# A decoder layer's mixer: the recurrence's gates of three chunks moved together behind the third query product

## The chip, the cores and the metric

The kernel runs on one core of one Trainium2 chip. The metric is the device time of one execution in microseconds (us). Before the change the median of 3 runs is 843.24 us (842.97 to 843.72). One more execution was profiled; it took 842.55 us, and its profile spans 840.8 us. Times inside the profile are counted from the start of that span.

Engines are named as in the profile: PE (TensorE matmuls), PEld (TensorE weight loads), DVE (VectorE), ACT (ScalarE), POOL (GpSimd), SP (SyncE, which here only issues DMAs). L1456 is line 1456 of the kernel before.

## The reference, cut to what matters

One layer: a half-step gated FFN, a mixer and a second half-step gated FFN, each between two RMS norms and added to the residual. SEQ is 512, D_MODEL 1024, float32 throughout. The mixer projects its input with one matrix `w_in` into the recurrence's input, its gate, and queries, keys and values, and runs two things side by side:

```python
def rg_lru(x_in, conv_w, conv_b, w_rg, b_rg, w_ig, b_ig, lam):
    xc = causal_depthwise_conv(x_in, conv_w, conv_b)
    r = jax.nn.sigmoid(block_diag(xc, w_rg, b_rg).astype(jnp.float32))
    i = jax.nn.sigmoid(block_diag(xc, w_ig, b_ig).astype(jnp.float32))
    log_a = LRU_C * r * jax.nn.log_sigmoid(lam.astype(jnp.float32))
    a = jnp.exp(log_a)
    mult = jnp.sqrt(-jnp.expm1(2.0 * log_a))
    u = mult * (i * xc.astype(jnp.float32))
    ...
    _, h = lax.associative_scan(combine, (a, u), axis=1)
```

and a sliding-window attention of 8 heads with 2 key/value heads (window 128, blocks of 128 queries, a sink term in the softmax). Both results are normed, joined and multiplied by `w_o`. The recurrence has 512 channels, four chunks of 128; `w_rg` and `w_ig` are block diagonal with blocks of 64.

## The kernel before, in words

**Layout and products.** Activations stand with channels on the 128 partitions and the 512 tokens along the free axis, so one chunk of 128 channels is one tile of 128x512. A float32 product is made of three matmuls: each operand is split into a rounded high part (a cast on ACT) and a low part (a subtraction on DVE or POOL), and high*high, high*low and low*high are summed in PSUM (`mm3`, L503 to L508). A projection chunk is eight such triples (`product`, L510), 24 matmuls into one PSUM bank. Weights come in by DMA (L175, on SP), are cast on ACT (L210, `whi`) and subtracted on DVE or POOL (L215, `wlo`); `W.take` hands them out and issues casts and loads some units ahead.

**What sets the order.** The schedule is by hand: each engine executes its instructions in the order in which the code issues them, and semaphores make an instruction wait for its inputs and for its output buffer. An engine whose next instruction waits does nothing else in the meantime. Buffers come from pools that are handed round in turn: 8 PSUM banks (`bank`), 38 tiles of 2 KB per partition (`t2k`), and 8 working buffers (`wt`). A tile asked for from a pool waits for the last reader of the buffer that it gets.

**The stage of the change** lies between 370 and 416 us. In order of the code:

- `in_product("pk")` and `in_product("pv")`: the products for keys and values. `conv_in` and `conv` (L1433, L1439) make the convolved chunks `xc` of the recurrence, on ACT and DVE.
- A loop over j = 0 to 3 with one query product `pq` each (24 matmuls). In the loop before the change follow, in this order: `split_xc(j + 1)` (L1472: `xch`, a cast on ACT, and `xcl`, a subtraction on POOL), `lru_gates(j)`, and `in_parts` for the queries (L1485).
- `lru_gates(ci)` (L1450) runs six matmuls of 64 rows by 512 columns, in pairs that use two halves of the array at once, into the banks `rg` and `ig`. ACT applies the sigmoid to each bank (`r`, L1458, and `other`, L1460). The tile `r` holds on its upper partitions the half that belongs to the other gate, so SP copies two halves into the buffer `ig` by DMA (L1459, L1461), POOL multiplies `xc` by it in place (L1463, the group `xc<-ig,xc`), and a DMA from POOL's queue puts the other half of the decay gate into `r` (L1464). The tile `th` is only asked for here; the decay writes it later.
- `in_parts` for query j (L1485): DVE scales the bank (`qT`, L1428), copies its first 128 columns to `home` (L1488), ACT casts the high part (`qT0h`, ..., L1494; for j = 3 the tile is a quarter of `attn`), and DVE subtracts the low part (`qT0l`, ..., L1495). For j = 3 that subtraction is put off (`deferred`, L186).
- After j = 0, PE transposes the values (`vt`, L1514) and DVE copies them to `home` (L1516).

Then attention begins: `preload(AF.Exp)` loads another function table on ACT (L482), and `products(0)` (L1598) multiplies the first block's queries and keys, straight from `home`: four steps of two matmuls, step j on the columns that query j was copied to. DVE masks the scores and takes the maxima, ACT takes the exponentials, PE transposes them (`pt`, L1653) and multiplies them by the values (`po`, L1676). Between these, PE works off the 96 matmuls of the gate projection (`gt`, `pump`), and ACT and DVE the decay of the recurrence: `decay_a` (L1561) writes `th`, `r` and `m`, `decay_b` (L1568), `root`, `root_u` and `scan` follow.

The function table for the sigmoid is loaded in front of the first sigmoid in ACT's order (the row ACT_TABLE_LOAD at L1458). The queue of SP is in order, and so is POOL's; POOL issues its DMAs itself, between its computations.

Of the kernel before, what the change touches and what calls it, by code (L numbers as in the profile page):

```python
# [23 lines left out]
KC = C // P  # L24
# [98 lines left out]
def tile_layer(ctx: ExitStack, tc: tile.TileContext, out: bass.AP, **ins: bass.AP):  # L123
    nc = tc.nc
    pe, dve, act, pool, sync = nc.tensor, nc.vector, nc.scalar, nc.gpsimd, nc.sync
# [14 lines left out]
    SIDE = [slice(0, HD), slice(HD, P)]  # L140

    def bank(name):
        return psum.tile([P, T], F32, tag="bank", name=name)

    def t2k(name, dt=F32):
        return big.tile([P, T], dt, tag="t2k", name=name, bufs=NT2K)
# [16 lines left out]
    def wt(name, w=T, dt=F32):  # L163
        return tmp.tile([P, w], dt, tag="w", name=name, bufs=NW)
# [5 lines left out]
    def load_raw(srcs, nk, w, name):  # L170
        raw = wpool.tile([P, nk * w], F32, tag="raw", name=f"raw_{name}", bufs=NRAW).rearrange("p (k c) -> p k c", k=nk)
        o = 0
        for src in srcs:
            n = src.shape[1]
            sync.dma_start(raw[:, :, o:o + n], src.rearrange("(k p) c -> p k c", p=P))  # L175
            o += n
        return raw
# [215 lines left out]
    for g, (f0, f1) in enumerate(GROUPS2):  # L393
        if g == 0:
            for f in range(f0, f1, 2):
                add_gate_up(w2, f, "b")
            r = W.raw(lambda f=f0: load_raw([ins["ffn2_w_down"][0, f * P:(f + 2) * P, :]], 2, D, f"bd{f}"))
# [40 lines left out]
    for i in range(2):  # L438
        load_x(0, i)
        for o in (0, F):  # L440
            r = first_raw[o, i] = t2k(f"first{o}{i}").rearrange("p (k c) -> p k c", k=4)
# [9 lines left out]
    for name, n in ROWS:  # L451
        if name in ("b_rg", "b_ig"):

            j = name == "b_ig"
# [37 lines left out]
    def col(name, i):  # L492
        return colrange(name)[:, i:i + 1]
# [930 lines left out]
    def in_product(name, hooks=(), ahead=AHEAD):  # L1424
        return product(W.take(ahead), mx.xs, name=name, hooks=hooks)
# [2 lines left out]
        dve.tensor_mul(t, b, R)  # L1428
        return t

    xcs, th, rs_, us_ = [], [], [], []

    def conv_in(ci, b):  # L1433
        xp = wt(f"xp{ci}", T + 4)
# [15 lines left out]
    def lru_gates(ci):  # L1450

        banks = bank(f"rg{ci}"), bank(f"ig{ci}")
        (hi, lo), (xh, xl) = gw["both"], xc_parts[ci]
        for i, (w, x) in enumerate(((hi, xh), (hi, xl), (lo, xh))):
            for ps, half in zip(banks, SIDE):
                pe.matmul(ps, w[half, ci, :], x[half, :], start=i == 0, stop=i == 2)  # L1456
        r, other, ig = t2k(f"r{ci}"), wt(f"other{ci}"), wt(f"ig{ci}")
        act.activation(r, banks[0], AF.Sigmoid, bias=col("b_rg", ci))  # L1458
        sync.dma_start(ig[SIDE[0], :], r[SIDE[1], :])  # L1459
        act.activation(other, banks[1], AF.Sigmoid, bias=col("b_ig", ci))  # L1460
        sync.dma_start(ig[SIDE[1], :], other[SIDE[0], :])  # L1461
        u = xcs[ci]
        pool.tensor_mul(u, ig, u)  # L1463
        pool.dma_start(r[SIDE[1], :], other[SIDE[1], :])  # L1464
        t = t2k(f"th{ci}")
        rs_.append(r)
        us_.append(u)
        th.append(t)

    xc_parts = {}  # L1470

    def split_xc(ci):  # L1472
        xh, xl = wt(f"xch{ci}", T, F32R), wt(f"xcl{ci}", T, F32R)
        act.copy(xh, xcs[ci])
        pool.tensor_sub(xl, xcs[ci], xh.bitcast(F32))
        xc_parts[ci] = xh, xl
# [8 lines left out]
    def in_parts(b, first, name, low=dve):  # L1485

        x = scaled(wt(name), b)
        dve.tensor_copy(first, x[:, :P])  # L1488
        if name == "qT3":
            spare.extend(fours("attn", F32R))  # L1490
            xh, xl = spare.pop(), spare.pop()
        else:
            xh, xl = t2k(f"{name}h", F32R), t2k(f"{name}l", F32R)
        act.copy(xh, x)  # L1494
        low.tensor_sub(xl, x, xh.bitcast(F32))  # L1495
        return xh, xl
# [7 lines left out]
    qT = []  # L1504
    for j in range(4):
        b = in_product(f"pq{j}")
        if j < KC - 1:
            split_xc(j + 1)
        lru_gates(j)
        qT.append(in_parts(b, q0[:, j * P:(j + 1) * P], f"qT{j}", deferred if j == 3 else dve))  # L1510
        if j == 0:
            vt = bank("vt")
            for b in range(NB):
                pe.transpose(vt[:, b * P:(b + 1) * P], vT[:, b * P:(b + 1) * P], ident)  # L1514
            v = home[0][:, P + 2 * T:P + 2 * T + 8 * (HD + 1)]
            dve.tensor_copy(v.rearrange("p (h d) -> p h d", d=HD + 1)[:, :, :HD], vt.rearrange("p (h d) -> p h d", d=HD))  # L1516
# [528 lines left out]
```

## Time and profile before

| | |
|---|---|
| median of 3 runs | 843.24 us (842.97 to 843.72) |
| profiled execution, its own time | 842.55 us |
| its span in the profile | 840.8 us |
| PE busy | 832.2 us (99%) |
| DVE busy | 723.8 us (86%) |
| ACT busy | 520.9 us (62%) |
| POOL busy | 162.6 us (19%) |

Busy time of an engine is the union of its instructions. In the lists in order of time each row has the start in us, the length in us, the engine, the source line, the operation, what it writes and reads, its shape and a count where equal rows are merged; a bracket gives the idle time of the engine just before and what ended it. Buffer numbers are left out of the names: `qT` stands for four tiles, one after the other. On ACT and DVE the start of an instruction can lie about 0.1 us before the end of the one ahead, since two overlap a little.

### The profile page before, as it was taken

Reading aid. Unit: us, or ns where it says so; the run is one execution under the profiler, and the core shown is the slowest. Engines: PE = TensorE matmul, PEld = TensorE weight load, DVE = VectorE, ACT = ScalarE, POOL = GpSimd, SP = SyncE. Lnnn points to the kernel's source line nnn. Section 1 sums busy time; section 2 is a strip of 40 time slices with the busy share of each in tenths; the row PEclk is TensorE's granted clock in tenths of the full one; section 3 lists DMA queues with packets and bytes.
Section 4 is the critical chain, followed back from the end, with each engine's and each line's share of the span. In section 5 each row is a group of like instructions: output and inputs, shape, how many; then the busy total and the mean of one; then the engine's idle time right before and its main releaser. Section 6 shows DMA issues by size and latency. Waiting matters only on the chain.

```text
span 840.8 us, 12378 instructions
## 1 busy us (share of the span) xinstructions
PE 832.2 (99%) x4504; PEld 718.9 (85%) x4504; DVE 723.8 (86%) x1026; ACT 520.9 (62%) x821; POOL 162.6 (19%) x178
## 2 busy tenths in 40 slices
PE   9999999999999999999999999999999999999996
PEld 8988888988988998987788899888888888888885
DVE  4978999998989965879889589799999899898996
ACT  6646756666666655556797456536758667666562
POOL 2023000140320333304531052002004114032001
PEclk9999999999999999999999999999999999999999
DMA  7249429398595799323511131169439939769842
GB/s 252 77 128 347 135 79 318 80 251 267 123 255 186 167 261 331 93 62 108 157 51 51 51 105 47 50 129 290 179 106 232 317 92 257 253 149 258 305 140 101
DMA packets 123614, 143.73 MB, mean 171 GB/s; under 512 B 23897, under 2 KB 81569, under 8 KB 123041
## 3 DMA queue, kind: packets, MB, share of 16 engines
q1 hardware_dynamic: 109232, 111.86, 42.0%
q0 software_dynamic: 14176, 30.94, 17.0%
q8 instruction: 35, 0.57, 0.3%
q14 instruction: 27, 0.21, 0.1%
q10 hardware_dynamic: 144, 0.13, 0.0%
HBM read 100.45 MB, written 40.89 MB: 168 GB/s over the span
## 4 chain that ended last, share of the span: by engine, by line
PE 96%; DVE 2%; DMA 1%; SPq 0%; issue 0%; ACT 0%; DVEq 0%; ACTq 0%
PE aa L951 10%; PE ab L951 10%; PE db L951 5%; PE da L951 5%; PE yaa L1347 3%; PE bb L951 3%; PE ba L951 3%; PE yda L1347 2%; PE ya L506 2%; PE ya L507 2%; PE ya L508 2%; PE aa L881 1%; PE a_first L1206 1%; PE yab L1884 1%; PE yab L1885 1%; PE yab L1886 1%
## 5 line engine op out<-in xcount | busy, mean ns | idle before, releaser
L1116 POOL DMA_DIRECT2D yp_a<-stage x42 | 36.8, 1064 | 182.6 <-ACT stage L1113 158.8
L1116 POOL DMA_DIRECT2D yp_b<-stage x42 | 36.4, 1084 | 144.3 <-ACT stage L1113 117.8
L506 PE MATMUL ya<-hha,whi_ad 128*128 128x512 f32 x62 | 24.1, 389 | 0.0
L507 PE MATMUL ya<-hla,whi_ad 128*128 128x512 f32 x62 | 24.1, 389 | 0.0
L508 PE MATMUL ya<-hha,wlo_ad 128*128 128x512 f32 x62 | 24.1, 389 | 0.0
L686 POOL TENSOR_TENSOR acca_r<-acca_r,sq_r 128x512 f32<-128x512 f32 x6 | 8.1, 1357 | 61.7 <-ACT sq_r L536 61.7
L1900 POOL DMA_DIRECT2D yp_b<-stage x8 | 4.3, 548 | 67.1 <-ACT stage L1899 67.1
L524 PE MATMUL an<-xh_mx,whi_xl 128*128 128x256 f32 x64 | 15.9, 289 | 0.0
L525 PE MATMUL an<-xh_mx,wlo_xl 128*128 128x256 f32 x64 | 15.5, 283 | 0.0
L2003 POOL TENSOR_TENSOR last<-yp,grow 128x512 f32<-128x512 f32 x3 | 3.9, 1290 | 57.2 <-DVE yp L1993 57.2
L2000 ACT ACTIVATE ysq<-yp 128x512 f32<-128x512 f32 (+1 forms) x8 | 4.8, 606 | 16.2 <-DVE yp L1993 16.2
L506 PE MATMUL gt<-xh_mx,whi_gt 128*128 128x512 f32 x32 | 14.3, 445 | 0.0
L508 PEld LDWEIGHTS ya<-hha,wlo_ad 128*128 128x128 f32 x62 | 11.6, 188 | 2.4
L506 PEld LDWEIGHTS ya<-hha,whi_ad 128*128 128x128 f32 x62 | 11.6, 188 | 2.4
L507 PEld LDWEIGHTS ya<-hla,whi_ad 128*128 128x128 f32 x62 | 11.6, 188 | 2.4
L536 ACT ACTIVATE sq_r<-yp_a 128x256 f32<-128x256 f32 (+1 forms) x10 | 5.0, 502 | 12.9 <-DVE yp_a L676 5.9
L506 PE MATMUL pq<-xh_mx,whi_q 128*128 128x512 f32 x32 | 12.8, 399 | 0.0
L506 PE MATMUL pub<-xh_f,whi_bu 128*128 128x512 f32 x32 | 12.6, 395 | 0.0
L508 PE MATMUL gt<-xh_mx,wlo_gt 128*128 128x512 f32 x32 | 12.6, 394 | 0.0
L506 PE MATMUL pgb<-xh_f,whi_bg 128*128 128x512 f32 x32 | 12.6, 393 | 0.0
L507 PE MATMUL gt<-xl_mx,whi_gt 128*128 128x512 f32 x32 | 12.6, 392 | 0.0
L508 PE MATMUL pgb<-xh_f,wlo_bg 128*128 128x512 f32 x32 | 12.5, 390 | 0.0
(2014 smaller groups left out, 3468.8 us busy)
## 6 DMA issues: line engine op xcount, KB each, us to landing
yp_a<-stage POOLq DMA_DIRECT2D x50, 256.0 KB, 9.1
yp_b<-stage POOLq DMA_DIRECT2D x50, 256.0 KB, 9.0
h_a<-za SPq DMA_DIRECT2D x16, 256.0 KB
hxa<-h_a SPq DMA_DIRECT2D x16, 256.0 KB
h_b<-zb SPq DMA_DIRECT2D x16, 256.0 KB
hxb<-h_b SPq DMA_DIRECT2D x16, 256.0 KB
xn<-in_x SPq DMA_DIRECT2D x8, 256.0 KB
xT_hbm<-xT POOLq DMA_DIRECT2D x2, 1024.0 KB, 9.8
```

What stands on the lines that cost most here:

```text
L506: pe.matmul(ps, hi[:, k, :], xh, start=start, stop=False)
L507: pe.matmul(ps, hi[:, k, :], xl, start=False, stop=False)
L508: pe.matmul(ps, lo[:, k, :], xh, start=False, stop=stop)
L524: pe.matmul(ps[:, sl], hi[:, k, :], xh, start=k == 0 and not goes_on, stop=False, skip_group_check=True)
L525: pe.matmul(ps[:, sl], lo[:, k, :], xh, start=False, stop=False, skip_group_check=True)
L881: pe.matmul(o, w[:, k, js], x, start=first and i + j + k == 0, stop=k == 3 and i == 2, skip_group_check=True)
L951: pe.matmul(b[tb], x[:, blk], w[:, k, :], start=first and q + k + j == 0, stop=q + k == 2 and j == 2, skip_group_check=True)
L1116: pool.dma_start(o, st.rearrange("p (a b) -> p a b", a=2) if len(o.shape) == 3 else st, accum_op=ALU.add)
L1206: pe.matmul(banks[j][:, HALF[0]], ws[j][part][:, k, :], n1.xs[k][xpart][:, HALF[0]], start=k == 0 and part == xpart, stop=stop and k == KD ...
L1347: pe.matmul(o, a[:, k, ms], x[:, js], start=first and i + k + m % 2 == 0, stop=k == 1 and i == 2, skip_group_check=True)
L1884: pe.matmul(banks[i], hh[:, js], hi[:, k, :], start=first and k == 0, stop=False, skip_group_check=True)
L1885: pe.matmul(banks[i], hh[:, js], lo[:, k, :], start=False, stop=False, skip_group_check=True)
```

## The change

`lru_gates` no longer takes a working buffer `ig`: the tile `th` of the same chunk is asked for at once, the two DMAs put the two halves into it, and POOL multiplies from it. The multiplication on POOL and the DMA behind it move into a function of their own, `gated_in`. In the loop over the query products, `split_xc` for chunks 1 and 2 stays behind query products 0 and 1, and no gates stand there. Behind query product 2 stand the gates of chunks 0 and 1, `split_xc(3)`, the gates of chunk 2, and `gated_in` for chunks 0, 1 and 2, all ahead of query 2's `in_parts`. Behind query product 3 stand the gates of chunk 3 and its `gated_in`.

```diff
-    xcs, th, rs_, us_ = [], [], [], []
+    xcs, th, rs_, us_, others = [], [], [], [], []
...
-        r, other, ig = t2k(f"r{ci}"), wt(f"other{ci}"), wt(f"ig{ci}")
+        r, other, ig = t2k(f"r{ci}"), wt(f"other{ci}"), t2k(f"th{ci}")
         act.activation(r, banks[0], AF.Sigmoid, bias=col("b_rg", ci))
         sync.dma_start(ig[SIDE[0], :], r[SIDE[1], :])
         act.activation(other, banks[1], AF.Sigmoid, bias=col("b_ig", ci))
         sync.dma_start(ig[SIDE[1], :], other[SIDE[0], :])
-        u = xcs[ci]
-        pool.tensor_mul(u, ig, u)
-        pool.dma_start(r[SIDE[1], :], other[SIDE[1], :])
-        t = t2k(f"th{ci}")
         rs_.append(r)
-        us_.append(u)
-        th.append(t)
+        us_.append(xcs[ci])
+        th.append(ig)
+        others.append(other)
+
+    def gated_in(ci):
+        pool.tensor_mul(us_[ci], th[ci], us_[ci])
+        pool.dma_start(rs_[ci][SIDE[1], :], others[ci][SIDE[1], :])
...
         b = in_product(f"pq{j}")
-        if j < KC - 1:
+        if j < 2:
             split_xc(j + 1)
-        lru_gates(j)
+        if j == 2:
+            lru_gates(0)
+            lru_gates(1)
+            split_xc(3)
+            lru_gates(2)
+            for ci in range(3):
+                gated_in(ci)
+        if j == 3:
+            lru_gates(3)
+            gated_in(3)
         qT.append(in_parts(b, q0[:, j * P:(j + 1) * P], f"qT{j}", deferred if j == 3 else dve))
```

## The prediction

> **What bounds the kernel now.** I read the busy shares first (PE 99%, in the table above), then the list of what PE waited for, then the engines one by one between 374 and 440 us in order of time. The whole list of PE's waits, with total, times and longest:
>
> ```profile
> PE warm L1193 <- POOL ident masks.py:199: 1.4, 1, 1.4
> PE xtp L1140 <- DMA xn<-in_x: 0.3, 1, 0.3
> PE rms_lru L550 <- DVE acc_lru L1800: 0.3, 1, 0.3
> ```
>
> That is all there is: PE loses 2.0 us to waits, none of it in the stage of the change (370 to 416 us). So time can be won here by taking work off PE alone, about as much as the gates' switching costs (below), and it is lost as soon as PE has to wait for anybody. The question is how far ACT, DVE and POOL, which bring PE its inputs, are from being late. ACT in this stage, in order of time:
>
> ```profile
> 391.16 1.28 ACT L1458 ACT_TABLE_LOAD   x1
> 392.45 0.69 ACT L1458 ACTIVATE r<-rg,cols 128x512 f32<-128x512 f32 x1
> 393.04 0.68 ACT L1460 ACTIVATE other<-ig,cols 128x512 f32<-128x512 f32 x1
> ...
> 400.66 0.62 ACT L1494 CAST qT1h<-qT 128x512 fp32r<-128x512 f32 x1 [0.56 <-DVE qT L1428]
> 401.19 1.04 ACT L210 CAST whi_gt<-raw_gt__4041 128x1024 fp32r<-128x1024 f32 x1
> 402.14 0.62 ACT L1474 CAST xch<-xc 128x512 fp32r<-128x512 f32 x1
> 402.66 0.68 ACT L1458 ACTIVATE r<-rg,cols 128x512 f32<-128x512 f32 x1
> 403.24 0.68 ACT L1460 ACTIVATE other<-ig,cols 128x512 f32<-128x512 f32 x1
> 405.06 0.62 ACT L1494 CAST qT2h<-qT 128x512 fp32r<-128x512 f32 x1 [1.14 <-DVE qT L1428]
> ...
> 409.12 0.69 ACT L1458 ACTIVATE r<-rg,cols 128x512 f32<-128x512 f32 x1 [2.48 <-PE ig L1456]
> ```
>
> Two things are to be seen. The table load and the first two sigmoids stand early, from 391.16 to 393.72, when ACT has next to nothing else that is ready: they cost nothing. And between query 1's cast at 400.66 and query 2's at 405.06 ACT does a weight cast, one `xch` and two sigmoids, then idles 1.14 us. DVE, whose low parts wait for those casts:
>
> ```profile
> 387.83 0.68 DVE L1428 TENSOR_TENSOR vT<-pv,R_mx 128x512 f32<-128x512 f32 x1
> ...
> 400.66 0.63 DVE L1488 COPY home<-qT 128x128 f32<-128x128 f32 x1
> ...
> 404.34 0.69 DVE L1428 TENSOR_TENSOR qT<-pq,R_mx 128x512 f32<-128x512 f32 x1 [1.19 <-POOL xc L1463]
> 405.06 1.15 DVE L1488 COPY home<-qT 128x128 f32<-128x128 f32 x1
> 406.13 0.68 DVE L1495 TENSOR_TENSOR qT2l<-qT,qT2h 128x512 fp32r<-128x512 f32 x1
> 406.73 1.21 DVE L215 TENSOR_TENSOR wlo_gt<-raw_gt__4041,whi_gt 128x1024 fp32r<-128x1024 f32 x1
> 408.23 0.69 DVE L1428 TENSOR_TENSOR qT<-pq,R_mx 128x512 f32<-128x512 f32 x1 [0.28 <-PE pq L508]
> 408.95 0.23 DVE L1488 COPY home<-qT 128x128 f32<-128x128 f32 x1
> ```
>
> The last row decides. That copy puts query 3 into `home`, and the last quarter of the first scores (`cur`) reads it. It ends at 409.18. On PE:
>
> ```profile
> 388.97 0.66 PE L1514 MATMUL vt<-ident,vT 128*128 128x128 f32 x4
> ...
> 394.48 0.39 PE L507 MATMUL pq<-xl_mx,whi_q 128*128 128x512 f32 x1
> 394.71 0.39 PE L508 MATMUL pq<-xh_mx,wlo_q 128*128 128x512 f32 x1
> ...
> 396.25 0.39 PE L507 MATMUL pq<-xl_mx,whi_q 128*128 128x512 f32 x1
> ...
> 408.92 1.05 PE L1598 MATMUL cur<-home 64*128 64x128 f32 x16
> ```
>
> The 16 rows of `cur` go in eight pairs over 1.05 us, 0.11 us apart, so the last quarter (two pairs) starts at 408.92 + 6 x 0.11 = 409.59. The copy was 0.41 us ahead of it. That is the slack against which the change is to be held.
>
> **The change, part by part.** *On PE nothing is added; two switches go.* From the last `pq` matmul ahead of a gates block (394.71) to the second one behind it (396.25) are 1.54 us. Matmuls of one shape follow each other by 0.23 us (394.48 to 394.71), so two steps of these would take 0.45, and the three pairs of gates 0.69; the remaining 0.40 us is the change between 128 and 64 rows. Three blocks standing together pay that once: 0.8 us less. But the transposes `vt` (388.97) now come straight behind query product 0, a block of about 1.0 us earlier, and their input `vT` ends on DVE at 387.83 + 0.68 = 388.51. PE waits there about 0.5 us. What is left is 0.1 to 0.3 us that PE is early at `cur`. No later wait lets it keep more.
>
> *On ACT the sigmoids move in front of query 2's cast.* Its order is now: cast of query 1, weight cast, table load, `r` and `other` of chunks 0 and 1, `xch` of chunk 3, `r` and `other` of chunk 2, cast of query 2. What leads up to 401.19 (DVE's convolution and queries 0 and 1) does not hang on the gates, so I leave it where it is. The weight cast ends at 402.23. The load takes 1.28: 403.51. Sigmoids follow each other by 0.58 (402.66 to 403.24): four take until 405.84. `xch` takes 0.52 (402.14 to 402.66): 406.36. Two more sigmoids: 407.52. Query 2's cast then runs from 407.52 to 408.14; before, it ended at 405.68. So 2.5 us late. The gates' banks are not late for this: PE is through with the three blocks about where block 2 ended before, at 402.5, and the second chunk's sigmoids start at 404.7. The early place of load and sigmoids was cover, and this cover is gone: 1.28 + 4 x 0.58 = 3.6 us more work in this stretch, against 1.14 us of idle time.
>
> *The buffers.* `th` is asked for earlier, from the pool of 2 KB tiles, and a late former reader would hold up SP's DMAs and the products on POOL behind them; the built program's semaphores for these DMAs name the sigmoids and DMAs long landed alone, so I count nothing.
>
> *On POOL the multiplications come behind `xcl` of chunk 3, and then in a row.* Its rows:
>
> ```profile
> 396.31 1.30 POOL L1463 TENSOR_TENSOR xc<-ig,xc 128x512 f32<-128x512 f32 x1 [3.78 <-DMA ig<-other]
> ...
> 399.01 2.19 POOL L1475 TENSOR_TENSOR xcl<-xc,xch 128x512 fp32r<-128x512 f32 x1 [0.90 <-ACT xch L1474]
> ...
> 406.84 2.27 POOL L1463 TENSOR_TENSOR xc<-ig,xc 128x512 f32<-128x512 f32 x1 [0.72 <-DMA ig<-other]
> ```
>
> An undisturbed one takes 1.30 us. One that starts while DVE subtracts two SBUF tiles waits for its end: DVE's subtraction ended at 406.73 + 1.21 = 407.94, POOL's at 409.11, 1.17 later. The other way about, DVE's copy at 400.66 took 0.63 instead of 0.23, and ended 0.09 after POOL's `xcl` (399.01 + 2.19 = 401.20). So they exclude each other. After the change `xch` of chunk 3 ends at 405.84 + 0.62 = 406.46, `xcl` runs to 407.8, and the product of chunk 0 from there to 409.1 (from the end of `other` to that product before: 393.72 to 396.31, 2.6 us; now 404.8 + 2.6 = 407.4, so the two DMAs are in time). Chunk 3's gates on PE want that `xcl` about where they stood, one step of `pq` and a block ahead of 408.92, near 408.2: 0.4 us of cover; every tenth beyond that would be a wait there, though one that the wait at `cur` swallows.
>
> *On DVE the low part of query 2 is what is held up.* It is in order ahead of `wlo_gt`, query 3 and its copy. It can start at 408.17, finds POOL at work until 409.1, and ends at 409.65 (0.68 less the 0.13 by which a blocked one was shorter). `wlo_gt` with 1.21 goes to 410.78. Query 3, which PE had ready long ago, is scaled from 410.70 to 411.39. Its copy starts at 411.42 and finds the product of chunk 1 on POOL, which waited for `wlo_gt` and ends at 410.78 + 1.17 = 411.95: it ends at 412.04. The wait on `qT` that goes (1.19 us at 404.34, for the buffer that POOL still read) gains nothing, since query 2's low part now waits for its cast.
>
> *The sum.* The last quarter of `cur` starts at 412.08 instead of 409.59: **2.5 us late**, of which PE waits about 2.7. Behind it stand all gate projections and the attention, whose scores, exponentials and masks start from `cur`, so ACT, DVE and POOL shift with it. What is late next: the product of chunk 3 and the DMA behind it leave POOL some 1.5 us later than now, which shifts with the attention's masks behind them. SP gets the six half-tile DMAs behind each other, and the next weight load comes behind them; the cast that wants it stands far behind in ACT's order, after the decay of three chunks. Both cost nothing in this sum; without that cover a late load would add its whole delay. The last wait of PE in the list (`rms_lru`, 0.3) could give back 0.3 at most, if DVE caught up; I take 0.
>
> The sum is made against the profiled execution, span 840.8 and time 842.55 us; the median of the runs shown lies 0.69 above that. With 2.5 us on the median: 843.24 + 2.5 = **845.7 us**, +0.30%.
>
> *Bounds of what the trace does not show.* Where POOL does not hold up DVE at all, query 2's low part ends at 408.85, `wlo_gt` at 409.98, query 3 at 410.59, the copy at 410.85: the last quarter at 410.9, +1.3. Where the product of chunk 1 gets in ahead of `wlo_gt` at 409.6 (both ask within 0.1 us, POOL after issuing its DMA), `wlo_gt` ends at 410.9 + 1.08 = 412.0, query 3 at 412.6, and the copy finds the product of chunk 2 at work to 413.2: +3.7. I take the middle, since DVE's next instruction starts 0.08 ahead of the end of the one before.
>
> *A rule against a row.* The table load's row is 1.28 us, and the sigmoid behind it starts 0.01 later (391.16 + 1.28 = 392.44, 392.45); the sum goes by that. The Trainium skill (ScalarE: Activation LUTs, "What ACT_TABLE_LOAD costs") counts about 1.38 us of draining on top of 1.28 for each switch of the table. By it, an estimate, query 2's cast would come 1.4 us later still and the time would be near 847.1. The trace does not agree: neither row has an idle bracket.
>
> **The rivals.** *Not slower (same):* PE's saving is what counts, because query 3's copy is early enough. It would be true if ACT reached query 2's cast some 2.7 us sooner than I add up. For it speaks that ACT idles 2.48 us at 409.12; against it that this idle time lies behind query 2's cast in the order, and the extra work ahead of it. Gain 0.1 to 0.3 us: 843.0 us. The whole switching saved, 0.8 us, would be 842.4; no wait of PE in this stage is there to be gained on top, so a gain over 0.2% has no source in the trace.
>
> *DVE held up less:* the bound of +1.3, 844.5 us. *DVE held up more:* the bound of +3.7, 846.9 us.
>
> *PE's clock falls in the wait.* While PE stands for 2.7 us its clock could drop, and then the matmuls behind it take twice as long for a while. The two last stretches of the span:
>
> ```profile
> 836.00:838.00 2.00, 0.00 (x0) 0.00 (x0) 1.34 (x3) 0.00 (x0) 0.00 (x0) 1.00 0.30 117
> 838.00:840.80 2.80, 0.00 (x0) 0.00 (x0) 0.00 (x0) 0.00 (x0) 0.00 (x0) 0.57 0.31 107
> ```
>
> PE (second column of busy time) does nothing in either; the clock (the column ahead of the DMA share) was still full through 2.0 idle us and was down in the next 2.8. Between these a wait of 2.7 us can go either way, 3.9 us sooner. If half a clock held for about the 2.8 us of that stretch, 1.4 us would be lost on top of 2.5 or 3.7: 847.1 to 848.3 us. The Trainium skill (TensorE: Matmul & The Clock Gate, "What's actually happening") puts the drop after an idle window of about 3.4 us and the return after a busy one as long; by it a 2.7 us wait stays at full clock and the longer one may not.
>
> **How the numbers follow.** Middle 0.50 (845.7); held up less 0.14 (844.5); held up more 0.20 with or without the clock, and the clock alone 0.05 (846.9 to 848.3); not slower 0.11 (842.4 to 843.2). A run to run difference of 0.2% (1.7 us, 841.6 to 844.9) is about what a measurement of this kernel can tell from no change. The case of +1.3 lies inside that, so same has 0.14 plus most of the 0.11, less the part of the former that comes out above: 0.16. Faster 0.03, slower 0.81. The range leaves out the best of the not slower cases and the clock's worst: 844.0 to 847.6.
>
> **What would show it.** In the profile after: the table load on ACT near 402.2 with the sigmoids behind it; query 2's cast at 407.5 with no idle time ahead; a new wait of PE at `cur` for DVE's copy to `home`, 2 to 3 us; a wait of about 0.5 at `vt`; one block of 18 gate matmuls instead of three. The prediction is wrong if that wait at `cur` is under 1 us, if the copy to `home` comes before 410, or if PE's clock dips behind it.

## The result, and the profile after

| | before | after |
|---|---|---|
| median | 843.23 us (842.97 to 843.72, 4 runs) | 848.12 us (847.92 to 848.89, 4 runs) |
| ratio | 1 | 1.0061, 95% interval 1.0049 to 1.0074 |
| profiled execution, its own time | 842.55 us | 848.04 us |
| its span | 840.8 us | 846.3 us |

The change costs 4.9 us of the median. The forecast was 2.5, with an upper end of 4.4.

Where the time went is on PE again. What PE waited for in the changed kernel (total, times, longest, in us; the two rows left out lie at the start of the span):

```profile
PE cur L1608 <- DVE home L1489: 3.5, 1, 3.5
...
PE vt L1524 <- DVE vT L1428: 0.5, 1, 0.5
...
PE rms_lru L550 <- DVE acc_lru L1810: 0.3, 1, 0.3
```

The two new waits are the two that were forecast, `cur` for the copy of query 3 and `vt`. But the one at `cur` is 3.5 us instead of 2.7. PE around it, in order of time (start, length, instruction; the bracket is the idle time ahead and what ended it):

```profile
409.22 0.83 PE L1608 MATMUL cur<-home 64*128 64x128 f32 x12
413.55 0.49 PE L1608 MATMUL cur<-home 64*128 64x128 f32 x4 [3.50 <-DVE home L1489]
...
414.77 0.62 PE L506 MATMUL gt<-xh_mx,whi_gt 128*128 128x512 f32 x1
```

A matmul of 128x512 takes 0.39 us elsewhere, and 0.62 from 414.77 on. That is the clock. The view by stretches, for PE alone (stretch, length, busy time of PE and its instructions, granted clock, share of the DMA engines, GB/s), cut where the trace records a change of the clock and in steps of 3.413 us ahead of it:

```profile
407.93:411.34 3.41, 2.12 (x21) 1.00 0.79 211
411.34:414.76 3.42, 1.21 (x7) 1.00 1.05 299
414.76:418.17 3.41, 3.41 (x9) 0.50 1.08 311
418.17:421.58 3.41, 3.41 (x32) 1.00 0.46 124
```

For 3.41 us, from 1.2 us after the end of the wait on, PE does half the work: 1.7 us lost.

Why the copy came so late stands on DVE and POOL. POOL's first row here lies ahead of the change; the same subtraction stands at 384.27 in the profile of before, so all times of after carry 0.36 us from the start of the program.

```profile
384.63 1.30 POOL L1476 TENSOR_TENSOR xcl<-xc,xch 128x512 fp32r<-128x512 f32 x1 [26.19 <-ACT xch L1475]
...
408.10 1.30 POOL L1468 TENSOR_TENSOR xc<-th,xc 128x512 f32<-128x512 f32 x1
409.34 0.56 POOL L1469 DMA_DIRECT2D r<-other  x1
409.91 1.28 POOL L1468 TENSOR_TENSOR xc<-th,xc 128x512 f32<-128x512 f32 x1
...
411.68 1.73 POOL L1468 TENSOR_TENSOR xc<-th,xc 128x512 f32<-128x512 f32 x1
```

```profile
408.43 1.52 DVE L1496 TENSOR_TENSOR qT2l<-qT,qT2h 128x512 fp32r<-128x512 f32 x1 [4.18 <-ACT qT2h L1495]
409.87 2.41 DVE L215 TENSOR_TENSOR wlo_gt<-raw_gt__4041,whi_gt 128x1024 fp32r<-128x1024 f32 x1
412.20 0.68 DVE L1428 TENSOR_TENSOR qT<-pq,R_mx 128x512 f32<-128x512 f32 x1
412.92 0.58 DVE L1489 COPY home<-qT 128x128 f32<-128x128 f32 x1
```

Read the two side by side. The low part of query 2 is held until POOL's product of chunk 0 ends. When it is through, at 409.95, POOL's product of chunk 1 has been there for 0.04 us, and goes first: `wlo_gt` takes 2.41 us instead of 1.21. Then `wlo_gt` holds the product of chunk 2 (1.73 instead of 1.30), and that one holds the copy (0.58 instead of 0.23).

The sum of the profile: the last quarter of `cur` starts at 413.55 instead of 409.59, 3.96 us later, of which 0.36 is the start: 3.6. With 1.7 for the clock that is 5.3, and 5.7 with the start; the spans differ by 5.5.

### The profile page after: what moved, and what is told of

The parts are those of the page before. It is cut to its first block, busy times and chain, and to the rows that moved or that the text cites. A ratio compares the mean times of both kernels' runs of the same rounds, so it can differ in the third digit from the quotient of the medians.

```text
span 846.3 us, 12374 instructions
## 1 busy us (share of the span) xinstructions
PE 834.0 (99%) x4504; PEld 720.3 (85%) x4504; DVE 723.6 (85%) x1026; ACT 520.8 (62%) x821; POOL 161.5 (19%) x178
## 4 chain that ended last, share of the span: by engine, by line
PE 92%; DVE 4%; ACT 1%; issue 1%; DMA 1%; SPq 0%; DVEq 0%; ACTq 0%
PE ab L951 10%; PE aa L951 10%; PE db L951 5%; PE da L951 5%; PE yaa L1347 3%; PE bb L951 3%; PE ba L951 3%; PE yda L1347 2%; PE ya L508 2%; PE ya L506 2%; PE ya L507 2%; PE aa L881 1%; PE a_first L1206 1%; PE yab L1896 1%; PE yab L1895 1%; PE yab L1894 1%
## 5 line engine op out<-in xcount | busy, mean ns | idle before, releaser
L1476 POOL TENSOR_TENSOR xcl<-xc,xch 128x512 fp32r<-128x512 f32 x4 | 6.0, 1494 | 39.2 <-ACT xch L1475 39.2
```

## The experiments

**The tile alone.** The kernel before, with the input gate put together in `th`:

```diff
-        r, other, ig = t2k(f"r{ci}"), wt(f"other{ci}"), wt(f"ig{ci}")
+        r, other, ig = t2k(f"r{ci}"), wt(f"other{ci}"), t2k(f"th{ci}")
...
-        t = t2k(f"th{ci}")
         rs_.append(r)
         us_.append(u)
-        th.append(t)
+        th.append(ig)
```

> The kernel before, its order untouched, with the input gate put together in the tile of the decay instead of a working buffer. My theory: the tile is of no account, the order of the gates is. The DVE wait of 1.19 us for POOL ahead of query 2 may go or stay, but PE has no wait there to lose. 843.2 us, ratio 0.999 to 1.001, no wait of PE between 370 and 416 us. Rival: the tile costs, because asking for it earlier makes the DMAs and the products on POOL wait for its last reader; then PE waits at `cur` or at chunk 3's gates and the time is 844.5 us or more.

Measured: 842.74 us, ratio 0.9993 (0.9984 to 1.0002), and no wait of PE in the stage. In the order of before the tile costs nothing; everything that follows is about the order.

**ACT's part: the table load back into idle time.** Two lines more behind `split_xc(1)` in the changed kernel:

```diff
+        if j == 0:
+            preload(AF.Sigmoid)
```

> The changed kernel with the sigmoid's function table loaded behind the split of chunk 1, in ACT's early idle time, instead of ahead of the first sigmoid. Theory A (the late cast of query 2 is what delays the copy of query 3, and the wait of 3.5 us brings the clock drop): the cast comes 1.28 us sooner, near 406.5, the wait of PE at `cur` falls to 1.2 to 2.2 us, the clock stays full, and the time is 844.5 to 845.5 us: of the 4.9 us that the change costs, 1.3 to 2.3 by the wait and 1.7 by the clock are gone. Theory B (the clock drop has nothing to do with the length of that wait): the clock still drops for 3 to 4 us near 415 us, time 846.2 to 847. Theory C (the subtractions of DVE and POOL that get in each other's way set the time, and ACT does not): the wait stays over 3 us and the time is near 848.1 us.

Measured: 846.86 us (844.74 to 847.92, 6 runs), ratio 1.0038 (1.0025 to 1.005). The cast came at 406.46, 1.29 us sooner, and the wait at `cur` fell from 3.5 to 2.1 us, as theory A has it. But the clock did not stay full, and the time lies in theory B's range, not in A's:

```profile
410.22:413.63 3.41, 1.34 (x8) 1.00 1.08 323
413.63:417.05 3.42, 3.42 (x10) 0.50 1.05 342
```

So a wait of 2.1 us can be enough for the fall. That it isn't always is argued from the times alone: one of the six runs took 844.74 us, the other five 846.69 to 847.92. Their mean clocks (0.999, and 0.996 to 0.997) fit, but don't prove it, since runs of the kernel before lie between 0.997 and 0.999 too.

**POOL's part: no products.** The changed kernel with this edit, which leaves the input gate of chunks 0 to 2 out of the computation:

```diff
-        pool.tensor_mul(us_[ci], th[ci], us_[ci])
+        if ci == 3:
+            pool.tensor_mul(us_[ci], th[ci], us_[ci])
```

> The changed kernel without POOL's multiplications by the input gate for chunks 0 to 2 (so the input gate is left out of three quarters of the recurrence's input); ACT's order and the DMAs stay. Theory A (POOL's products hold up DVE's two subtractions and the copy): query 2's cast ends at 408.4 as in the changed kernel, `wlo_gt` takes 1.2 instead of 2.41 us, the copy of query 3 comes near 411, PE waits 1.3 us at `cur` instead of 3.5, the clock stays full, and the time is 844.5 us (844.0 to 845.2). Theory C' (ACT's late cast alone makes the wait): the wait stays at 3 us or more, with the clock drop behind it, 847.5 us or more.

Measured: 844.05 us, ratio 1.0009 (1.0000 to 1.0018), a wait of 1.1 us at `cur`, the clock full. DVE's rows in this run:

```profile
408.73 0.69 DVE L1497 TENSOR_TENSOR qT2l<-qT,qT2h 128x512 fp32r<-128x512 f32 x1 [4.17 <-ACT qT2h L1496]
409.34 1.22 DVE L215 TENSOR_TENSOR wlo_gt<-raw_gt__4041,whi_gt 128x1024 fp32r<-128x1024 f32 x1
...
411.20 0.23 DVE L1490 COPY home<-qT 128x128 f32<-128x128 f32 x1
```

The cast of query 2 is as late as in the changed kernel (its times lie 0.3 us behind those of the changed kernel from the start on), yet each of the held instructions has its undisturbed length again. The late cast alone costs 1.1 us of waiting; the other 2.4 of the 3.5 are POOL's products, and with them goes the fall of the clock.

**The clock by itself.** The kernel before, with the scaling of query 3 repeated n times on DVE, so that the copy is late and nothing ahead of it is moved:

```diff
         x = scaled(wt(name), b)
+        if name == "qT3":
+            for i in range(n):
+                scaled(x, b)
```

> The kernel before with nothing moved: DVE repeats the scaling of query 3 three times (the same values into the same tile, about 0.64 us each) ahead of the copy to `home`, so that PE waits at `cur` for about 1.9 us. It asks what a wait there costs by itself, and from what length on the clock follows. Theory A (the wait costs its length, and the clock falls for 3.4 us, 1.7 us of loss, once the wait is about 2 us or longer): 845.3 us in runs where the clock stays and 847.0 us where it falls; both may come, since the changed kernel with the early table load had a wait of 2.1 us and runs from 844.7 to 847.9. Theory B (the fall belongs to the changed kernel's order of work, not to the wait): clock full in every run, 845.3 us.

> As the run with three repeats, with five: a wait of about 3.2 us at `cur`, near the 3.5 us of the changed kernel. Theory A: the clock falls to half for 3.4 us behind it in every run, 3.2 + 1.7 = 4.9 us: 848.3 us, the time of the changed kernel from a cause put in by hand. Theory B: 846.6 us with the clock full.

> As before, with seven repeats: a wait of about 4.5 us at `cur`. Theory A with one fall of fixed length: 4.5 + 1.7 = 6.2 us, 849.6 us. Theory A' (the half clock lasts longer behind a longer wait, or comes already in the wait): 851 us or more, or under 849 if most of the half clock lies inside the wait. Theory B: 847.9 us with the clock full.

| n | wait at `cur` | median (range), 4 runs each | ratio (95%) | mean clock of the runs |
|---|---|---|---|---|
| 3 | 1.7 | 846.52 (845.09 to 847.08) | 1.0038 (1.0023 to 1.0053) | 0.998, 0.997, 0.997, 0.996 |
| 5 | 3.1 | 846.84 (846.24 to 847.25) | 1.0044 (1.0029 to 1.0059) | 0.997, 0.998, 0.998, 0.997 |
| 7 | 4.6 | 850.01 (849.39 to 850.46) | 1.0081 (1.0066 to 1.0096) | 0.995 in all |

Theory B falls: the clock goes down in the order of before as well. Theory A's "in every run" hardly holds for n = 5: the fall stands in the profiled run, but A's time was 848.3 us, and the two fastest runs (846.24 and 846.47) lie near the 846.6 of a full clock. That is argued from the times, since only one run of each has a trace. PE in stretches of 3.41 us, for n = 3, n = 5 and n = 7:

```profile
406.60:410.02 3.42, 2.77 (x24) 1.00 0.78 263
410.02:413.43 3.41, 2.40 (x13) 1.00 0.80 226
```

```profile
407.24:410.65 3.41, 2.19 (x21) 1.00 0.66 213
410.65:414.06 3.41, 1.51 (x9) 1.00 0.93 281
414.06:417.48 3.42, 3.42 (x10) 0.50 0.46 142
```

```profile
409.67:413.08 3.41, 0.00 (x0) 1.00 0.71 180
413.08:416.49 3.41, 2.28 (x8) 0.50 0.84 281
416.49:419.91 3.42, 3.42 (x10) 0.50 0.02 5
```

In every trace here all recorded changes of the clock are whole multiples of 3.413 us apart (832.85 in the profile of before, for instance, is 244 of them): the time is cut into windows whose edges have nothing to do with the kernel's work. Of the windows, those with PE busy for 1.21, 1.34 and 1.51 us are followed by half a clock, those with 2.12, 2.19 and 2.40 are not. A wait of 1.7 us split by an edge does nothing (n = 3, the profiled run). The other three runs of n = 3 took 1.3 to 2.0 us longer, so one that lies within a window may be enough; no trace shows it. For n = 7 the clock falls 1.1 us ahead of the wait's end, and the window after the fall, busy for 2.28 us, doesn't bring it back; the full one does. Its span agrees: 4.6 + (6.83 - 1.13) / 2 = 7.4, and 848.2 - 840.8 = 7.4. So the half clock came in the wait and lasted longer, as A' has it, though the time lies outside both of its ranges and near A's 849.6. The Trainium skill (TensorE: Matmul & The Clock Gate, "What's actually happening") has the same free-running window of 3413 ns. It puts the fall after an idle window; the traces differ there, since windows in which PE was busy for up to 1.51 us have it too.

**Query 2 first.** The changed kernel with `lru_gates` split into its matmuls (`gate_products`) and the rest (`gate_sigmoids`), and the scaling, cast and subtraction of query 2 issued between them; the 18 gate matmuls stay together:

```diff
         if j == 2:
-            lru_gates(0)
-            lru_gates(1)
-            split_xc(3)
-            lru_gates(2)
             for ci in range(3):
-                gated_in(ci)
+                gate_products(ci)
...
         qT.append(in_parts(b, q0[:, j * P:(j + 1) * P], f"qT{j}", deferred if j == 3 else dve))
+        if j == 2:
+            split_xc(3)
+            for ci in range(3):
+                gate_sigmoids(ci)
+            for ci in range(3):
+                gated_in(ci)
```

> The changed kernel with query 2's scaling, cast and subtraction issued ahead of the sigmoids and the products on POOL, right behind the three chunks' gate matmuls; PE's block of 18 gate matmuls stays as it is. Theory A (what costs is ACT's work ahead of query 2's cast, not the grouping of the gates on PE): the cast of query 2 comes near 403, the copy of query 3 before 410, and the wait at `cur` is gone or under 0.5 us; the exponentials of the first block come later on ACT, so that PE gets a new wait of 0.9 to 1.3 us at the transposes `pt`; clock full; 843.2 to 845.0 us. Rival D (the grouping itself costs: the later sigmoids delay the decay and the attention whatever the queries do): a wait of 2 us or more turns up elsewhere and the time stays over 846 us.

Measured: 844.93 us, ratio 1.0019 (1.0010 to 1.0029), the clock full in the profiled run. No wait at `cur`; in its place 0.6 at `pt` and 0.8 at `po`. So two thirds of the cost (0.61% to 0.19%) go with issuing query 2 ahead of the sigmoids and the products. What is left is new lateness behind it, which the next two runs were to remove.

**Both mends, and `vt` later.** The last run with the table load of early_load, and then also with the second edit:

```diff
+        if j == 0:
+            preload(AF.Sigmoid)
...
-        if j == 0:
+        if j == 1:
             vt = bank("vt")
```

> Both mends together in the changed kernel: the sigmoid's table loaded behind the split of chunk 1, and query 2 ahead of sigmoids and products. Theory A (ACT's work ahead of query 2's cast, and the sigmoids' lateness ahead of the first exponentials, are all that the change costs): no wait of PE at `cur`, the waits at `pt` and `po` under 0.3 us each, 0.5 us left at `vt`, clock full; 842.9 to 843.6 us, as before. Rival D (the grouping costs by itself): a wait of 1 us or more is left at `pt` or `po`, 844.3 us or more.

> As the run with both mends, with the transposes `vt` one query product later. The wait of 0.5 us at `vt` goes as well. Theory A: no wait of PE between 380 and 420 us over 0.3 us; the 0.8 us of switching that the grouping saves on PE come through: 842.3 to 843.0 us. Rival D': the saving is used up by waits at `pt` or `po`: 843.2 to 844 us.

Measured: 844.88 us, ratio 1.0021 (1.0011 to 1.0030), and 844.93 us, ratio 1.0022 (1.0013 to 1.0031). Neither comes to the time of before, as theory A had it both times. Rival D holds. D' is right about the wait at `pt`, 1.4 us in both, but its range ends 0.9 us lower. In the second the wait at `vt` is gone as meant, and others stand in its place (0.5 us at `cur`, 0.4 at `sc`, 0.3 at `pq`). In the first of them POOL and DVE stand like this:

```profile
410.32 1.29 POOL L1472 TENSOR_TENSOR xc<-th,xc 128x512 f32<-128x512 f32 x1
...
412.11 1.29 POOL L1472 TENSOR_TENSOR xc<-th,xc 128x512 f32<-128x512 f32 x1
```

```profile
410.53 3.44 DVE L1636 COPY_PREDICATED cur<-up,home 128x512 f32<-128x512 uint8 x1 [0.65 <-PE cur L1617]
```

```profile
PE pt L1672 <- ACT sc L1662: 1.4, 1, 1.4
```

The products in a row now stand where the attention masks its first scores: 3.44 us instead of 0.70, and PE waits for the exponentials behind. To see whether that is all, the version with the later `vt` and the edit of no_products:

> The run with both mends and the later `vt`, without POOL's multiplications by the input gate for chunks 0 to 2 (left out of the computation as in the earlier run without products). That run still lay 1.8 us above the kernel before, with a mask on DVE of 3.44 us instead of 0.70 and a wait of 1.4 us at `pt` behind it. Theory P (what is left of the cost is the three products in a row on POOL, at the place where the attention's first mask wants to run): the mask takes 0.7 us, the wait at `pt` goes, and the 0.8 us of switching that the grouping saves on PE show: 842.0 to 842.8 us. Theory D (the grouping costs in another way too): 843.5 us or more.

Measured: 846.39 us (844.16 to 848.83, 4 runs, mean clocks 0.999 to 0.995), ratio 1.0053 (1.0034 to 1.0073). Theory P is half right: the mask takes 0.70 us and the wait at `pt` is gone. But it isn't faster; one more wait has come up in the profiled run, which is the fastest of the four. What makes the others up to 4.7 us longer has no trace; a mean clock of 0.995, that of the runs with n = 7, suggests that the clock fell in them.

```profile
PE po L1696 <- POOL pa L1680: 1.9, 1, 1.9
```

```profile
417.85 1.29 POOL L1473 TENSOR_TENSOR xc<-th,xc 128x512 f32<-128x512 f32 x1 [6.53 <-DMA th<-other]
...
419.63 2.13 POOL L1680 TENSOR_SCALAR_AFFINE_SELECT pa<-pa 128x512 f32<-128x512 f32 x2
```

POOL's mask `pa` stands behind the product of chunk 3, and that product waits for its half-tile DMA until 417.85. In the kernel before it ran 4.9 us sooner:

```profile
412.94 1.29 POOL L1463 TENSOR_TENSOR xc<-ig,xc 128x512 f32<-128x512 f32 x1 [3.35 <-DMA ig<-other]
```

In the eleven profiles in which the three chunks' gates stand together, that product starts between 415.0 and 418.8; with the order of before it starts at 412.9, and at 412.7 in the run with the tile alone. So the lateness goes with the grouping. DMAs were slower here. From issue to landing (last number, median in us, between 395 and 420 us) those of POOL's queue took, in the kernel before and in this run:

```profile
r<-other POOLq DMA_DIRECT2D x4, 128.0 KB, 2.8
```

```profile
r<-other POOLq DMA_DIRECT2D x4, 128.0 KB, 4.9
```

The changed kernel has 6.0 there. And SP issued a weight load right ahead of chunk 3's half tiles in this run (in the kernel before it stood at 404.56, 5.3 us ahead of them):

```profile
409.27 0.59 SPq L175 DMA_DIRECT2D raw_wo__4261<-in_w_o  x1
...
410.71 0.55 SPq L1465 DMA_DIRECT2D th<-other  x1
```

That six half tiles and the load now crowd each other is argued from these rows, not shown by a run of its own. What is shown is that the grouping makes this product late, and that with the other waits gone PE waits for it: a third cost, which the wait at `cur` had hidden.

**Who goes first, DVE or POOL.** The changed kernel with POOL's instructions for chunks 0, 1 and 2 in four other orders, all else equal. With P for the product and D for the DMA, the changed kernel has P0 D0 P1 D1 P2 D2. The edit of the first, dma_ahead (P0 D0 D1 P1 D2 P2):

```diff
-            for ci in range(3):
-                gated_in(ci)
+            gated_in(0)
+            for ci in (1, 2):
+                pool.dma_start(rs_[ci][SIDE[1], :], others[ci][SIDE[1], :])
+                pool.tensor_mul(us_[ci], th[ci], us_[ci])
```

The same lines stand as P0 D0 D1 P1 P2 D2 in dma_ahead2, P0 D0 D1 D2 P1 P2 in dmas_first, and P0 P1 P2 D0 D1 D2 in dmas_last.

> The changed kernel with the DMA from POOL's queue of chunks 1 and 2 issued ahead of the product of the same chunk instead of behind it. So POOL asks for its product of chunk 1 about 0.5 us later, after DVE's `wlo_gt` has begun. Theory A (the two exclude each other, and who has asked when the other ends goes next): `wlo_gt` now takes 1.2 us instead of 2.41, ahead of the product; the copy of query 3 is held by that product to about 412.4, PE waits 2.3 us at `cur` instead of 3.5: the order on which my prediction was built, and 2.5 us later than before by the wait alone. The clock as behind the other wait of this length: it mostly falls, 847.3 us, or 845.8 where it does not. Rival E (POOL goes first whoever asks): `wlo_gt` still takes 2.4 us, wait 3.5 us or more, 848 us or more.

> The changed kernel with all three DMAs from POOL's queue behind the product of chunk 0 and ahead of the products of chunks 1 and 2. POOL thus issues DMAs for about 1.6 us before it comes to its next product, while DVE has `wlo_gt` (1.2 us) ready. It asks what held `wlo_gt` for 4.71 us in the run with two DMAs ahead. Theory F (a product that is ready on POOL keeps DVE out already while POOL still issues the DMAs in front of it, and DVE comes in only when POOL has nothing ready): `wlo_gt` starts only behind both products, near 413.4, takes 4 us or more, PE waits 5 us, 849.5 us or more. Theory A (DMA issue does not hold DVE, and turns are taken): `wlo_gt` takes 1.2 us between 409.9 and 411.1, PE waits about 2.3 us, 845.8 us with the clock full and 847.3 with a fall.

> The changed kernel with the three products on POOL straight behind each other and the three DMAs behind them. Theory F: between products that are all ready DVE does not come in at all: query 2's low part takes over 3 us and runs behind the third product, near 412; `wlo_gt` and query 3 behind it, PE waits 4 us or more, 849 us or more. Theory A (turns): the low part of query 2 runs behind the first product, `wlo_gt` behind the second, as in the changed kernel; wait 3 to 3.7 us, 847.5 to 848.5 us.

> As the run with the DMAs ahead of the products of chunks 1 and 2, but with the DMA of chunk 2 moved behind its product, so that no DMA is issued between the products of chunks 1 and 2. There DVE's `wlo_gt` was passed over twice, by the product of chunk 1 and by that of chunk 2. Theory G (it is the DMA between two products that lets POOL go on without letting DVE in): `wlo_gt` runs behind the product of chunk 1, takes 2.9 us instead of 4.71, PE waits about 3.6 us. Theory H (passed over for another reason): 4 us or more, PE waits about 5 us.

| order | `wlo_gt` took | wait at `cur` | half clock in the profiled run | time |
|---|---|---|---|---|
| changed kernel | 2.41 | 3.5 | 3.41 us | 848.12 |
| dma_ahead | 4.71 | 5.4 | 6.83 us | 849.87, ratio 1.0080 (1.0063 to 1.0096) |
| dma_ahead2 | 4.18 | 4.9 | 6.83 us | 849.87 (one run) |
| dmas_first | 1.21 | 2.3 | none | 845.48 (one run) |
| dmas_last | 2.28 | 3.4 | 6.83 us | 848.70 (one run) |

With all DMAs in front (dmas_first), `wlo_gt` gets in ahead of the product. DVE, and POOL beside it:

```profile
410.15 1.21 DVE L215 TENSOR_TENSOR wlo_gt<-raw_gt__4041,whi_gt 128x1024 fp32r<-128x1024 f32 x1
...
412.00 0.61 DVE L1489 COPY home<-qT 128x128 f32<-128x128 f32 x1
```

```profile
410.17 1.06 POOL L1517 DMA_DIRECT2D r<-other  x2
411.24 2.51 POOL L1519 TENSOR_TENSOR xc<-th,xc 128x512 f32<-128x512 f32 x2
```

That is the order on which the forecast was built, with a wait of 2.3 us where it had 2.7, and 845.48 us is the forecast's time to 0.2, in one run. Theory F falls in the form in which it was put, since `wlo_gt` ran while POOL issued two DMAs; whether a product behind a single DMA keeps DVE out, this doesn't tell. With one DMA in front (dma_ahead), it went the other way:

```profile
409.18 0.54 POOL L1517 DMA_DIRECT2D r<-other  x1
409.74 1.28 POOL L1518 TENSOR_TENSOR xc<-th,xc 128x512 f32<-128x512 f32 x1
410.94 0.54 POOL L1517 DMA_DIRECT2D r<-other  x1
411.48 1.28 POOL L1518 TENSOR_TENSOR xc<-th,xc 128x512 f32<-128x512 f32 x1
```

```profile
409.14 4.71 DVE L215 TENSOR_TENSOR wlo_gt<-raw_gt__4041,whi_gt 128x1024 fp32r<-128x1024 f32 x1
```

`wlo_gt` was next on DVE from 409.23, half a microsecond before POOL's product began, and still it ended only at 413.85, 1.09 us behind the end of the second product (412.76). Rival E predicted the first loss, nobody the second. Taking the DMA between the two products away (dma_ahead2) changes nothing in that, so theory G falls. In the changed kernel, in early_load (2.43) and in dmas_last (2.28) DVE came in after one product. What decides it stays open.

## Why the prediction was wrong

*Right: what moves the time, and where.* PE's idle time at `cur`, for DVE's copy of query 3, is the cost. Query 2's cast was put at 407.52 and came at 407.75, or 407.39 without the 0.36 from the start; the wait at `vt` was put at 0.5 and is 0.5; the low part of query 2 was to end at 409.65 and ended at 409.95 (409.59). The table load costs its row and nothing on top here too: the changed kernel has

```profile
402.49 1.28 ACT L1458 ACT_TABLE_LOAD   x1
403.79 0.69 ACT L1458 ACTIVATE r<-rg,cols 128x512 f32<-128x512 f32 x1
...
407.75 0.65 ACT L1495 CAST qT2h<-qT 128x512 fp32r<-128x512 f32 x1
```

with the first sigmoid 0.02 us behind it. PE's saving left 0.06 us at the start of `cur` (409.22 - 0.36 against 408.92), a little under the 0.1 to 0.3 forecast.

*Wrong, first: "I take the middle".* The choice that DVE goes first at 409.6 failed. POOL went first, and then everything came as the bound of +3.7 has it: `wlo_gt` was to end at 412.0 and ended at 411.92 (start taken off), the copy at 413.2 and 413.14; +3.6 measured. The reason given for the middle, that DVE's next instruction starts 0.08 us ahead of the end of the one before, was no reason: the row of `wlo_gt` starts at 409.87 here, 0.04 us ahead of the row of the product (409.91) that passed it. What mattered was which engine was through first behind POOL's first product, which ended at 409.40: POOL's DMA issue took until 409.90, DVE's low part until 409.95, nearly a tie. The runs show that it isn't even settled by who is there first. With both ends so far apart, 0.50 against 0.20 was too sure.

*Wrong, second: the clock.* "The clock's worst" was left out of the range, and the clock's fall counted only as part of 0.20 and 0.05. It cost 1.7 us, the price that the rival had to within 0.3. The failing step was to read the rows at the end of the span as a time without work after which the clock falls, between 2.0 and 4.8 us. Even that time was misread: in the profile of before PE's last matmul ends at 834.23, so the clock, which fell at 838.42, had stayed full through 4.2 us without work, not 2.0. The hold runs show another quantity: the share of work in a fixed window of 3.41 us. By it the length of a wait of two or three us doesn't decide alone: in the traces the clock stayed full behind waits of 1.7 and 2.3 us, and fell behind 2.1 and 3.1 and all longer ones. The forecast's own 2.7 us lies in between, so the fall belonged in the range, with a weight near one half (an estimate from these few traces). The rival "held up more, with the clock" (up to 848.3) is what happened.

*Costed at nothing, and hidden: SP's queue and the half-tile DMAs.* In the changed kernel no wait of PE hangs on them. With the wait at `cur` mended and the products gone they are late next (6.53 us on POOL, then 1.9 us at `po`), so the cover was the lateness ahead of them. The forecast had chunk 3's product 1.5 us later than before; in the changed kernel it came 3.4 us later (416.68 - 0.36 against 412.94).

*The rival "not slower"* needed query 2's cast 2.7 us sooner. Moving it there (query first) gave 844.93 us, not 843.0: its gain was used up by waits at `pt` and `po`.

## What to carry to other kernels

Where work is grouped to save switches on the busiest engine, look at what stood spread out on the other engines and now stands in a row: here three POOL products and six sigmoids hit the start of the attention, and so, as far as is argued, do six DMAs. A wait of PE of about 2 us or more can cost another 1.7 us beside its own length (2.1 us did, 2.3 us did not), so price it with and without. Where two engines exclude each other and both are ready within some tenths, carry both orders to the end and let the range hold both.

## What the runs showed of the hardware

- PE's clock is decided per window of 3.413 us: a window at full clock with PE busy for 1.51 us or less was followed by half a clock; one with 1.89 us (dmas_first, the row below), and at the end of the n = 5 run one with 1.62 us (837.32 to 840.73), was not. Behind the waits it came back after a full window, not after one busy for 2.28 us (n = 7) or 2.44 (dmas_last). The edges lie elsewhere in each run, so a wait of 2.3 us cost nothing beside itself (dmas_first) and one of 2.1 us cost 1.7 more (early_load).

```profile
408.45:411.86 3.41, 1.89 (x20) 1.00 0.80 231
```

- DVE operations with two SBUF inputs, and its SBUF copies, waited for a POOL product to end and then ran in full. The Trainium skill (SBUF — State Buffer, "SBUF: two separate sides") describes such a lock, held for a whole instruction by whoever starts first. The rows agree that one waits for the other's end. They don't agree on who goes first, if the start of a row is meant: in dma_ahead the row of `wlo_gt` starts 0.6 us ahead of the product's and ends behind both products. Nor is it a simple turn: DVE came in after one product (2.41, 2.43, 2.28 us) or after two (4.71, 4.18 us, and a mask of 3.44).
